# Self-attention scores of two heads in the upper and lower 64 rows of the TensorE array

## The chip, the cores and the metric

The kernel runs on one core of a Trainium2 chip. The metric is the device time of one execution in microseconds (us). The kernel before takes 815.65 us, the median of three runs (815.26 to 817.07).

## What is computed

One layer of an encoder for 512 tokens of width 1024: a token mixer, a cross-attention into 256 memory tokens and a gated MLP with a convolution, each between two RMS norms. The token mixer has two halves that run side by side: a recurrent group of four heads (HGRN2) and the self-attention group that this change touches. It has eight query heads of 64 elements that share two key and value heads, so heads 0 to 3 use the first key head and heads 4 to 7 the second:

```python
def axial_gqa_attention(q, k, v):
    ...
    scale = ATT_HEAD_DIM ** -0.5

    def one_block(qblk):
        s = jnp.einsum("bqhgd,bkhd->bhgqk", qblk, k).astype(jnp.float32) * scale
        p = jax.nn.softmax(s, axis=-1).astype(v.dtype)
        return jnp.einsum("bhgqk,bkhd->bqhd", p, v)
```

## The kernel before

**Splitting.** Matmul operands are kept as two fp32r tiles: `hi`, the value rounded by a cast on ScalarE (ACT), and `lo`, the rest, by a subtraction on VectorE (DVE) (`split`, L120 to L122). An ordinary product is then three matmuls, hi*hi, hi*lo and lo*hi (`mm3`, L277 to L280).

**Queries and keys.** `rope_q` (L770) writes for each block of 128 tokens and each head a row of 128 elements: 64 of `hi`, then 64 of `lo`. `turn_q` (L776) transposes them on TensorE (PE), so that `qT` holds one head in all 128 partitions, `hi` in the upper 64 and `lo` in the lower 64. The keys (`put_kv`, `turn_k`) are written twice, so that `kT` holds the same key `hi` (index c = 0) or the same key `lo` (c = 1) in both halves of the partitions.

**Attention** (L865 to L916) is a generator of 35 steps. Step i makes the scores of one head and one block of 128 queries: two matmuls with 128 rows and 512 columns into one PSUM bank `ps_s` (L872), which together give all four products of hi and lo. Then `softmax` (L847): the maximum of each row on DVE (L850), the exponential with its sum on ACT (L853), the reciprocal on DVE (L854), and the scaling, two times of three on ACT (L858), else on DVE (L860). Two steps later `turn(i - 2)` transposes the probabilities with four matmuls into a bank `ps_o` (L882), and `split` writes them as `hi` (ACT L121) and `lo` (DVE L122) to two `big` tiles of their head. When a head's four blocks are done, `weigh` (L885) multiplies them with the values, eight matmuls (L893), and ACT and DVE (L897, L898) write the result out.

**What sets the order.** `weave` (L73) interleaves three generators at L945 by the amounts that they yield: the last recurrent head (`hgrn_core(3)`), `attention`, and `attention_filler`. The filler is other PE work: the keys (`proj_fm`, 256 columns, banks `ps_b`, L278 to L280) and values of the cross-attention, and the first half of the output projection. From what is written in this order the framework's scheduler makes its own order for each engine, fixed when the kernel is built. Each engine works through its list in order, so a waiting instruction holds up all that stand behind it on that engine.

**Room.** There are two banks for each of the tags `s`, `o`, `b` and `c`, and 16 `big` buffers. A `big` tile is given room that an earlier tile has left; its first writer waits for the last reader of that tile. `hgrn_core(3)` has three such tiles: `qk` (queries and keys, multiplied in place, level by level), `tt` (the products of the gates) and `room`. For each of its levels it makes four matmuls into `ps_c` (L647; L654 at the level of 128), two multiplications on DVE (L673) and a masked copy (L679); then it transposes the keys (L659) and goes on with L664 and L685 to L687.

Of the kernel before, what the change touches and what calls it, by code (L numbers as in the profile page):

```python
# [10 lines left out]
F32R = mybir.dt.float32r  # L11
# [7 lines left out]
P = 128  # L19
D = 1024  # L20
T = 512
NB = T // P
# [67 lines left out]
def layer(tc, io, out):  # L90
    nc = tc.nc
# [13 lines left out]
    def small():  # L105
        return sm.tile([P, 16], F32, name="small", tag="small")

    def bank(tag):
        return ps.tile([P, 512], F32, name="ps_" + tag, tag=tag)

    def big(shape, dt=F32):
        return b8.tile(shape, dt, name="big", tag="big")

    def tmp2(shape=(P, 512), dt=F32, tag="ta"):
        return t2.tile(list(shape), dt, name="tmp2", tag=tag, bufs=TMP_BUFS[tag])

    def tmp4(shape, dt=F32):
        return t4.tile(shape, dt, name="tmp4", tag="tmp4")

    def split(hi, lo, src, eng=None):  # L120
        nc.scalar.copy(hi, src)  # L121
        (eng or nc.vector).tensor_sub(lo, src, hi.bitcast(F32))  # L122
# [159 lines left out]
    def blk(b):  # L282
        return slice(b * P, (b + 1) * P)
# [209 lines left out]
    for j in range(4):  # L493
# [8 lines left out]
        for k in range(2):  # L502
            kc = 2 * j + k
            for a, w in ((0, wh), (0, wl), (1, wh)):
                for b in range(NB):
                    nc.tensor.matmul(v_ps[b], hT.get(kc, blk(b))[a], w[:, half(k)],
                                     start=kc == 0 and a == 0 and w is wh, stop=kc == 7 and a == 1)
# [58 lines left out]
    def pair(act, i):  # L566
        t = big([P, 2, 2, T], F32R)
        act.hi[i], act.lo[i] = t[:, 0], t[:, 1]
# [200 lines left out]

    def rope_q(b, z):  # L770
        qr = norm_rope(z, 8, 0, b)
        qs = tmp4([P, 8, 2, 64], F32R)
        split(qs[:, :, 0, :], qs[:, :, 1, :], qr)
        return qs.rearrange("p h a d -> p h (a d)")

    def turn_q(b, q3):  # L776
        for g in range(2):
# [65 lines left out]
    kT, vv, qT = qkv["kT"], qkv["vv"], qkv["qT"]  # L843
# [3 lines left out]
    def softmax(s, n, width):  # L847
        s3 = s.rearrange("p (n k) -> p n k", n=n)
        mx = small()
        nc.vector.tensor_reduce(mx[:, :n], s3, axis=AX.X, op=ALU.max, negate=True)  # L850
        e = tmp2((P, n, width), tag="tq")
        for i in range(n):
            nc.scalar.activation(e[:, i, :], s3[:, i, :], ACT.Exp, bias=mx[:, i:i + 1], accum_out=mx[:, 2 + i:3 + i])  # L853
        nc.vector.reciprocal(mx[:, 4:4 + n], mx[:, 2:2 + n])  # L854
        for i in range(n):
            scaled[0] += 1
            if scaled[0] % 3:
                nc.scalar.mul(e[:, i, :], e[:, i, :], mx[:, 4 + i:5 + i])  # L858
            else:
                nc.vector.tensor_scalar(e[:, i, :], e[:, i, :], mx[:, 4 + i:5 + i], None, op0=ALU.mult)  # L860
        return e
# [3 lines left out]
    def attention():  # L865
        probs, pts, atts = {}, {}, {}

        def scores(i):
            h, qb = divmod(i, 4)
            s = bank("s")  # L870
            for c in range(2):
                nc.tensor.matmul(s, qT[h // 4][:, h % 4, blk(qb)], kT[:, 2 * (h // 4) + c, :],  # L872
                                 start=c == 0, stop=c == 1)
            probs[i] = softmax(s, 1, 512)

        def turn(i):
            if i % 4 == 0:
                pts[i // 4] = [big([P, 4, T], F32R) for _ in range(2)]
            (hi, lo), e = pts[i // 4], probs.pop(i)
            o = bank("o").rearrange("p (k n) -> p k n", k=4)  # L880
            for c in range(4):
                nc.tensor.transpose(o[:, c, :], e[:, 0, blk(c)], ident)  # L882
            split(hi[:, :, blk(i % 4)], lo[:, :, blk(i % 4)], o)

        def weigh(h):  # L885
            pt = pts.pop(h)
            if h % 2 == 0:
                atts[h // 2] = tmp2()
            att = atts[h // 2]
            o = bank("o")  # L890
            for c in range(4):
                for j in range(2):
                    nc.tensor.matmul(o, vv[:, c, h // 4].rearrange("p a d -> p (a d)"), pt[j][:, c, :],  # L893
                                     start=c + j == 0, stop=c == 3 and j == 1)
            low, high = slice(0, 64), slice(64, 128)
            dst, oth = (low, high) if h % 2 == 0 else (high, low)
            nc.scalar.copy(att[dst, :], o[oth, :])  # L897
            nc.vector.tensor_add(att[dst, :], o[dst, :], att[dst, :])  # L898
            if h % 2:
                if h % 4 == 1:  # L900
                    pair(mix, h // 4)
                split(*mix.get(h // 2, slice(0, T)), att)
                att_done[0] += 1

        n = 8 * NB
        yield ATT_LEAD
        while not turned[0]:
            yield None
        for i in range(n + 3):
            if i < n:  # L910
                scores(i)
            if 2 <= i <= n + 1:
                turn(i - 2)
            if i % 4 == 2 and i > 4:
                weigh(i // 4 - 1)
            yield 1.1  # L916

    def put_kx(c):
# [279 lines left out]
    rows = [small() for _ in range(NB)]  # L1198
# [148 lines left out]
```

## Time and profile before

| what | value |
|---|---|
| median of 3 runs | 815.65 us |
| profiled execution, first to last instruction (span) | 813.8 us |
| PE busy in the span | 803.3 us |
| DVE, ACT, POOL busy in the span | 574.7, 482.1, 136.9 us |
| first and last start of the score matmuls (L872) | 211.7 and 300.3 us |
| last start of the weighing matmuls (L893) | 308.9 us |

PE is a matmul, PEld a weight load beside it. A row of a timeline gives the start, the duration, the engine, the line, the operation, the tiles written and read, and the count. A row of a group gives the line, engine and operation, the tiles and shapes, the count, then the busy time in us with the mean of one in ns, then the idle time ahead of them with what ended it. The ends of matmuls are modelled and overlap the next start; what one costs PE is the distance from its start to the next one's. The profiled execution's own span is 1.85 us shorter than the median of the runs.

### The profile page before, as it was taken

What the parts mean: (1) busy time and instruction counts of PE and PEld (TensorE: products, weight loads), DVE (VectorE), ACT (ScalarE), POOL (GpSimd) and SP (SyncE); (2) the same over time, 40 slices, a digit from 0 to 9 for tenths busy, and PEclk for the clock granted to TensorE, in tenths of its full rate; (3) what the DMA queues carried; (4) which work ended last, traced back from release to release, by engine and by line L of the source; (5) the groups of instructions that cost most, each with busy time, mean ns of one, the idle gap of its engine ahead of it and who ended that gap; (6) DMA issues with size and microseconds to landing.
All of it is one profiled execution on the core that took longest, in us unless ns stands there. A gap on an engine that the chain in (4) does not pass through costs nothing.

```text
span 813.8 us, 11771 instructions
## 1 busy us (share of the span) xinstructions
PE 803.3 (99%) x4426; PEld 691.0 (85%) x4426; DVE 574.7 (71%) x868; ACT 482.1 (59%) x796; POOL 136.9 (17%) x213
## 2 busy tenths in 40 slices
PE   9999999999999999999999999999999999999996
PEld 7888888889998887888888898899999998888885
DVE  5456587469886865855453767987777788888765
ACT  5675757459988874644543553665555545566651
POOL 0111201053233102301010311211111111000301
PEclk9999999999999999999999999999999999999999
DMA  8685645569899753256634158776665677278852
GB/s 296 202 259 139 160 103 117 118 159 247 229 250 254 182 172 126 78 181 157 180 117 142 33 164 208 154 200 166 179 171 143 150 200 178 91 208 278 239 130 104
DMA packets 42457, 139.61 MB, mean 172 GB/s; under 512 B 5280, under 2 KB 6560, under 8 KB 42400
## 3 DMA queue, kind: packets, MB, share of 16 engines
q1 hardware_dynamic: 28944, 97.43, 35.5%
q0 software_dynamic: 12160, 38.54, 26.2%
q10 hardware_dynamic: 1296, 2.89, 1.0%
q8 instruction: 34, 0.56, 0.3%
q14 instruction: 23, 0.19, 0.1%
HBM read 135.17 MB, written 25.17 MB: 197 GB/s over the span
## 4 chain that ended last, share of the span: by engine, by line
PE 92%; DVE 3%; ACT 2%; issue 1%; POOL 1%; DMA 0%; DVEq 0%; POOLq 0%; SPq 0%; ACTq 0%
PE ps_b L279 10%; PE ps_b L280 10%; PE ps_b L278 10%; PE ps_s L278 6%; PE ps_s L280 6%; PE ps_s L279 6%; PE ps_o L278 5%; PE ps_o L279 5%; PE ps_o L280 5%; PE ps_c L278 5%; PE ps_c L280 5%; PE ps_c L279 5%; PE ps_c L647 3%; PE ps_o L893 2%; PE ps_s L872 2%; PE ps_o L882 2%
## 5 line engine op out<-in xcount | busy, mean ns | idle before, releaser
L222 ACT CAST wh<-raw 128x1024 fp32r<-128x1024 f32 x110 | 113.7, 1035 | 114.6 <-PE ps_b L279 35.3
L224 DVE TENSOR_TENSOR wl<-raw,wh 128x1024 fp32r<-128x1024 f32 (+1 forms) x77 | 92.3, 1201 | 72.2 <-ACT wh L222 72.0
L278 PE MATMUL ps_b<-big,wh 128*128 128x512 f32 (+1 forms) x344 | 122.3, 355 | 0.0
L280 PE MATMUL ps_b<-big,wl 128*128 128x512 f32 (+1 forms) x344 | 121.2, 352 | 0.0
L279 PE MATMUL ps_b<-big,wh 128*128 128x512 f32 (+1 forms) x344 | 121.2, 352 | 0.0
L280 PEld LDWEIGHTS ps_b<-big,wl 128*128 128x128 f32 x344 | 65.1, 189 | 8.5 <-DMA wl<-in_wu_dram 0.2
L278 PEld LDWEIGHTS ps_b<-big,wh 128*128 128x128 f32 x344 | 65.1, 189 | 8.3
L279 PEld LDWEIGHTS ps_b<-big,wh 128*128 128x128 f32 x344 | 65.1, 189 | 8.1
L673 DVE TENSOR_TENSOR big<-big 128x512 f32<-128x512 f32 x64 | 47.2, 755 | 9.6 <-PE ps_c L647 4.0
L278 PE MATMUL ps_s<-wh,big 128*128 128x512 f32 (+1 forms) x140 | 53.4, 383 | 0.0
L279 PE MATMUL ps_s<-wl,big 128*128 128x512 f32 (+1 forms) x140 | 53.3, 381 | 0.0
L280 PE MATMUL ps_s<-wh,big 128*128 128x512 f32 (+1 forms) x140 | 53.0, 379 | 0.0
L230 POOL DMA_DIRECT2D wl<-in_w_dram x33 | 29.3, 887 | 126.7 <-ACT wl L229 91.5
L122 DVE TENSOR_TENSOR big<-ps_o,big 128x512 fp32r<-128x512 f32 x54 | 36.9, 687 | 15.0 <-ACT big L121 13.4
L121 ACT CAST big<-ps_o 128x512 fp32r<-128x512 f32 x54 | 31.7, 588 | 18.5 <-PE ps_o L996 7.5
L278 PE MATMUL ps_s<-big,wh 128*128 128x256 f32 (+1 forms) x120 | 40.0, 334 | 0.0
L279 PE MATMUL ps_s<-big,wh 128*128 128x256 f32 (+1 forms) x120 | 40.0, 333 | 0.0
L280 PE MATMUL ps_s<-big,wl 128*128 128x256 f32 (+1 forms) x120 | 40.0, 333 | 0.0
L278 PE MATMUL ps_o<-wh,big 128*128 128x512 f32 (+1 forms) x102 | 39.2, 385 | 0.0
L279 PE MATMUL ps_c<-big,wh 128*128 128x256 f32 (+1 forms) x120 | 39.1, 326 | 0.0
L278 PE MATMUL ps_c<-big,wh 128*128 128x256 f32 (+1 forms) x120 | 39.1, 326 | 0.0
L280 PE MATMUL ps_c<-big,wl 128*128 128x256 f32 (+1 forms) x120 | 39.1, 326 | 0.0
(315 smaller groups left out, 2149.3 us busy)
## 6 DMA issues: line engine op xcount, KB each, us to landing
raw<-in_w_dram SPq DMA_DIRECT2D x91, 512.0 KB, 3.6
wl<-in_w_dram POOLq DMA_DIRECT2D x33, 512.0 KB, 7.3
sum_t<-in_wd_dram SPq DMA_DIRECT2D x20, 512.0 KB, 6.3
tmp<-in_wu_dram SPq DMA_DIRECT2D x14, 512.0 KB, 6.9
sum_t<-in_wd_dram POOLq DMA_DIRECT2D x10, 512.0 KB, 8.4
sum_t<-sum_t POOLq DMA_DIRECT2D x10, 512.0 KB, 7.5
big<-sum_t SPq DMA_DIRECT2D x10, 512.0 KB, 4.7
raw<-sum_t SPq DMA_DIRECT2D x10, 512.0 KB, 4.4
```

The lines of the kernel that those rows point to most:

```text
L121: nc.scalar.copy(hi, src)
L122: (eng or nc.vector).tensor_sub(lo, src, hi.bitcast(F32))
L222: nc.scalar.copy(wh, raw)
L224: last_low[0] = nc.vector.tensor_sub(wl[:, :by_dma], raw[:, :by_dma], wh[:, :by_dma].bitcast(F32)).ins
L230: nc.gpsimd.dma_start(wl[:, by_dma:], source(i)[:, by_dma:], accum_op=ALU.add)
L278: nc.tensor.matmul(o, a[0], b[0], start=start, stop=False, skip_group_check=again)
L279: nc.tensor.matmul(o, a[0], b[1], start=False, stop=False, skip_group_check=again)
L280: last_mm[0] = nc.tensor.matmul(o, a[1], b[0], start=False, stop=stop, skip_group_check=again).ins
L647: nc.tensor.matmul(o[:, b, :], kc[:, blk(b)], qc[:, blk(b)] if m == 1 else pat(qk, b * P, [[2 * m, P // (2 * m)], [T + m, 2], [1, m]]), st ...
L673: nc.vector.tensor_tensor(out=c, in0=c, in1=pat(tt, toff + off, [[2, npair], [gap, 2], [0, m]]), op=ALU.mult)
L872: nc.tensor.matmul(s, qT[h // 4][:, h % 4, blk(qb)], kT[:, 2 * (h // 4) + c, :], start=c == 0, stop=c == 1)
L882: nc.tensor.transpose(o[:, c, :], e[:, 0, blk(c)], ident)
```

## The change

- `rope_q` writes the rotated queries as all eight heads' `hi`, then all eight heads' `lo`, so that a row of 128 elements that `turn_q` transposes holds two heads. `qT[0]` then holds `hi` and `qT[1]` holds `lo`, each with head 2n in the upper 64 partitions and head 2n + 1 in the lower 64.
- `scores(i)` works on a pair of heads and one block of queries. It takes both `ps_s` banks, one for each head, and issues three products for each (hi*hi, hi*lo, lo*hi; lo*lo is left out), alternating between the heads. Each matmul has 64 rows and 512 columns; in the built program its array tile is 64x128, at row 0 for the first head and row 64 for the second. Every other matmul of the kernel keeps the 128x128 tile. There are 96 score matmuls where 64 were.
- `turn` and `weigh` work on the same amounts as before, but a pair of heads is in flight at once, so four `big` tiles of probabilities are made at the first block of a pair where two were made at the first block of a head. The turns come one step after the scores, one head ahead of the next scores and one behind them.
- The generator has 16 such steps and a last one, each yielding twice, and weighs the last two heads at its end.

```diff
--- before.py
+++ after.py
@@ -769,9 +769,9 @@
 
     def rope_q(b, z):
         qr = norm_rope(z, 8, 0, b)
-        qs = tmp4([P, 8, 2, 64], F32R)
-        split(qs[:, :, 0, :], qs[:, :, 1, :], qr)
-        return qs.rearrange("p h a d -> p h (a d)")
+        qs = tmp4([P, 2, 8, 64], F32R)
+        split(qs[:, 0], qs[:, 1], qr)
+        return qs.rearrange("p a (h two) d -> p (a h) (two d)", two=2)
 
     def turn_q(b, q3):
         for g in range(2):
@@ -866,17 +866,21 @@
         probs, pts, atts = {}, {}, {}
 
         def scores(i):
-            h, qb = divmod(i, 4)
-            s = bank("s")
-            for c in range(2):
-                nc.tensor.matmul(s, qT[h // 4][:, h % 4, blk(qb)], kT[:, 2 * (h // 4) + c, :],
-                                 start=c == 0, stop=c == 1)
-            probs[i] = softmax(s, 1, 512)
-
-        def turn(i):
+            n, qb = divmod(i, 4)
+            both = [bank("s") for _ in range(2)]
+            for a, c in ((0, 0), (0, 1), (1, 0)):
+                for k in range(2):
+                    rows = slice(64 * k, 64 * k + 64)
+                    nc.tensor.matmul(both[k], qT[a][rows, n, blk(qb)], kT[rows, 2 * (n // 2) + c, :],
+                                     start=a + c == 0, stop=a == 1)
+            for k in range(2):
+                probs[i, k] = softmax(both[k], 1, 512)
+
+        def turn(i, k):
+            h = 2 * (i // 4) + k
             if i % 4 == 0:
-                pts[i // 4] = [big([P, 4, T], F32R) for _ in range(2)]
-            (hi, lo), e = pts[i // 4], probs.pop(i)
+                pts[h] = [big([P, 4, T], F32R) for _ in range(2)]
+            (hi, lo), e = pts[h], probs.pop((i, k))
             o = bank("o").rearrange("p (k n) -> p k n", k=4)
             for c in range(4):
                 nc.tensor.transpose(o[:, c, :], e[:, 0, blk(c)], ident)
@@ -902,17 +906,25 @@
                 split(*mix.get(h // 2, slice(0, T)), att)
                 att_done[0] += 1
 
-        n = 8 * NB
+        n = 4 * NB
         yield ATT_LEAD
         while not turned[0]:
             yield None
-        for i in range(n + 3):
+        for i in range(n + 1):
+            if i % 4 == 1 and i > 4:
+                weigh(i // 2 - 2)
+            if i > 0:
+                turn(i - 1, 0)
             if i < n:
                 scores(i)
-            if 2 <= i <= n + 1:
-                turn(i - 2)
-            if i % 4 == 2 and i > 4:
-                weigh(i // 4 - 1)
+            yield 1.1
+            if i % 4 == 1 and i > 4:
+                weigh(i // 2 - 1)
+            if i > 0:
+                turn(i - 1, 1)
+            yield 1.1
+        for h in (6, 7):
+            weigh(h)
             yield 1.1
 
     def put_kx(c):
```

The order on three engines shows what the scheduler makes of this. In the names, `big_1159` holds the transposed keys, `big_1161` and `big_1162` the transposed queries, `big_1120` and `big_1121` the memory tokens, `ps_s` banks are told apart by number. First PE, a few us into the attention, with the score matmuls of the third block. Before, each bank has both its matmuls in one row:

```order
L872 MATMUL ps_s_2067<-big_1159,big_1161 128x512 x2
L279 MATMUL ps_b_2143<-big_1121,wh_1912 128x256
L872 MATMUL ps_s_2085<-big_1159,big_1161 128x512 x2
L280 MATMUL ps_b_2143<-big_1120,wl_1913 128x256
L278 MATMUL ps_b_2143<-big_1120,wh_1912 128x256
L882 MATMUL ps_o_2078<-ident_84,tmp2_2054 128x128 x4
```

Now, with the pair's two banks `ps_s_2131` and `ps_s_2132`:

```order
L874 MATMUL ps_s_2131<-big_1159,big_1161 128x512 x2
L874 MATMUL ps_s_2131<-big_1159,big_1162 128x512
L279 MATMUL ps_b_2160<-big_1121,wh_1912 128x256
L280 MATMUL ps_b_2160<-big_1120,wl_1913 128x256
L278 MATMUL ps_b_2160<-big_1120,wh_1912 128x256
L279 MATMUL ps_b_2160<-big_1121,wh_1912 128x256
L874 MATMUL ps_s_2132<-big_1159,big_1161 128x512
L886 MATMUL ps_o_2124<-ident_84,tmp2_2088 128x128 x4
L874 MATMUL ps_s_2132<-big_1159,big_1161 128x512
L874 MATMUL ps_s_2132<-big_1159,big_1162 128x512
```

The pair is not kept together here: the scheduler puts a matmul where its own bank comes free, so the first head's three stand ahead of the second head's three, with other work between. Of the 16 pairs, six alternate unbroken, two alternate with four transposes between them, four have three matmuls and then three (one of these with a weighing between and the order mixed at its end), and four are taken apart as here.

Second, PE where the last levels of `hgrn_core(3)` stand. Before, the level of 128 (L654) lies between the filler's matmuls:

```order
L279 MATMUL ps_b<-big,wh 128x256
L280 MATMUL ps_b<-big,wl 128x256
L654 MATMUL ps_c<-big 128x128 x4
L278 MATMUL ps_b<-big,wh 128x256
L279 MATMUL ps_b<-big,wh 128x256
L280 MATMUL ps_b<-big,wl 128x256
L278 MATMUL ps_b<-big,wh 128x256
L279 MATMUL ps_b<-big,wh 128x256
L280 MATMUL ps_b<-big,wl 128x256
L872 MATMUL ps_s<-big 128x512 x2
L882 MATMUL ps_o<-ident,tmp_2375 128x128 x4
```

Now the level of 64 (L647), the level of 128 and what follows stand one behind the other:

```order
L280 MATMUL ps_b<-big,wl 128x256
L647 MATMUL ps_c<-big,tmp_2351 128x128 x4
L654 MATMUL ps_c<-big 128x128 x4
L659 MATMUL ps_c<-ident,big 128x128 x4
L664 MATMUL ps_c<-big 128x128
L886 MATMUL ps_o<-ident,tmp_2141 128x128 x4
L664 MATMUL ps_c<-big 128x128
L886 MATMUL ps_o<-ident,tmp_2147 128x128 x4
L664 MATMUL ps_c<-big 128x128 x2
L685 MATMUL ps_c<-big 128x128
L874 MATMUL ps_s<-big 128x512
L886 MATMUL ps_o<-ident,tmp_2223 128x128 x4
```

The next filler matmul comes nine rows further down, behind the first weighing (L897). Moved here are the filler, which stood between these steps and is now used up ahead of them, and the turns of the third block (`tmp_2141`, `tmp_2147`), which now stand behind them.

Third, DVE at the same place. Before, the `lo` halves of the probabilities (`big_2380`, that head's) and the last level's multiplications (L673, in place on `qk`, which is `big_1411`, with the gates `tt`, which is `big_1412`) take turns:

```order
L673 TENSOR_TENSOR big_1411<-big_1411,big_1412 128x2x2x128
L854 RECIPROCAL small_2429<-small_2429 128x1
L122 TENSOR_TENSOR big_2380<-ps_o_2435,big_2379 128x4x128
L860 TENSOR_SCALAR tmp2_2431<-tmp2_2431,small_2429 128x512
L673 TENSOR_TENSOR big_1411<-big_1411,big_1412 128x2x2x128
L850 TENSOR_REDUCE small_2465<-ps_s_2462 128x1
L122 TENSOR_TENSOR big_2380<-ps_o_2471,big_2379 128x4x128
```

Now (`big_2099` is the `lo` tile of the second head, `big_2070` that of the first):

```order
L850 TENSOR_REDUCE small_2302<-ps_s_2294 128x1
L673 TENSOR_TENSOR big_1411<-big_1411,big_1412 128x4x2x64
L679 COPY_PREDICATED big_1849<-masks_299,ps_c_2353 128x4x128
L673 TENSOR_TENSOR big_1411<-big_1411,big_1412 128x2x2x128 x2
L122 TENSOR_TENSOR big_2099<-ps_o_2100,big_2098 128x4x128
L122 TENSOR_TENSOR big_2099<-ps_o_2176,big_2098 128x4x128
L122 TENSOR_TENSOR big_2070<-ps_o_2206,big_2069 128x4x128
```

The second head's `lo` halves have moved behind the last L673: in the built program `big_2099` lies at the address of `big_1412`, the gates, whose last reader is that L673. Until then the banks `ps_o_2100` and `ps_o_2176`, both that there are, stay taken. In the same way the second tile of cross-attention keys (`big_2159`) lies at the address of the first head's `hi` probabilities and waits for the first weighing, as it did before (there for the `lo` probabilities); that weighing stood behind the scores of 8 blocks of a head and now stands behind 11, and behind all these steps. Outside the stretch from the turning of the queries to the end of the attention, the lists of PE, DVE, ACT and POOL are the same as before; on SP one load of weights changes places with the loads of `x`.

## The prediction

> **What bounds the kernel now.** I read the page first, for the engine that has no room.
>
> ```profile
> span 813.8 us, 11771 instructions
> PE 803.3 (99%) x4426; PEld 691.0 (85%) x4426; DVE 574.7 (71%) x868; ACT 482.1 (59%) x796; POOL 136.9 (17%) x213
> PE 92%; DVE 3%; ACT 2%; issue 1%; POOL 1%; DMA 0%; DVEq 0%; POOLq 0%; SPq 0%; ACTq 0%
> ```
>
> PE is busy for 99% of the span, and 92% of the chain that ended last is PE. So an edit is worth what it takes from PE's list, or puts into it, waits included. Next the busy times of the attention's own stretch, from the first score matmul to the end of the last weighing, and the waits on PE from 211 to 311 us.
>
> ```profile
> 211.70:309.10 97.40, 97.04 (x574) 82.94 (x575) 72.85 (x144) 79.37 (x164) 20.54 (x23) 1.00 0.78 217
> PE ps_b L278 <- DVE big L122: 0.3, 1, 0.3
> ```
>
> After the stretch's length, the busy times are PE, PEld, DVE, ACT and POOL; then the clock, which is full. PE is idle for 97.40 - 97.04 = 0.36 us of 97, and one wait makes 0.3 of it. Nothing is to be won by better hiding. DVE and ACT, at 75% and 81%, have little slack: if their work bunches up, PE will wait.
>
> A busy PE is not yet a price, since matmuls overlap. The timeline gives prices, as distances between starts:
>
> ```profile
> 286.93 2.04 PE L893 MATMUL ps_o<-big,vv 128*128 128x512 f32 x8
> 288.81 0.39 PE L280 MATMUL ps_b<-wh,big 128*128 128x512 f32 x1
> 289.03 0.62 PE L872 MATMUL ps_s<-big 128*128 128x512 f32 x2
> 289.49 0.60 PE L882 MATMUL ps_o<-ident,tmp 128*128 128x128 f32 x4
> 289.85 0.48 PE L278 MATMUL ps_c<-wh,big 128*128 128x512 f32 x1
> 290.16 0.40 PE L279 MATMUL ps_c<-wl,big 128*128 128x512 f32 x1
> 290.40 0.39 PE L280 MATMUL ps_c<-wh,big 128*128 128x512 f32 x1
> ...
> 240.81 0.28 PE L279 MATMUL ps_b<-big,wh 128*128 128x256 f32 x1
> 240.93 0.28 PE L280 MATMUL ps_b<-big,wl 128*128 128x256 f32 x1
> 241.05 1.05 PE L654 MATMUL ps_c<-big 128*128 128x128 f32 x8
> 241.86 0.36 PE L278 MATMUL ps_b<-big,wh 128*128 128x256 f32 x1
> ```
>
> A score matmul costs (289.49 - 289.03) / 2 = 0.23 us, four transposes 0.36, a weighing 1.88, a filler matmul of 256 columns 0.12, four matmuls of the recurrence 0.81 (0.20 each; L647, L664, L685 and L686 are taken at this). The first matmul behind the transposes takes 0.31 to the next start where its kind takes 0.23 or 0.24: a change of kind costs some 0.08.
>
> **The slots of the score matmuls.** Before, 64 matmuls cost 64 x 0.23 = 14.7 us. After, there are 96 of half the rows. If a matmul in the upper rows and one in the lower run side by side, a pair of heads needs 3 slots in place of 4, 48 in all, and 3.7 us would be won. But by the order only neighbours can run side by side. A slot is counted where a score matmul follows one on the same rows, or follows other work. The six unbroken pairs need 3 slots each, 18. Those with three and then three share only the two in the middle: 5 each for four pairs, 20. The two with transposes between need 4 each, 8. The four that are taken apart need 6 each, 24. Sum 70, six more than before: 6 x 0.23 = +1.4 us. The edit's own arithmetic is gone before any wait is counted. No row of before has 64 rows or two matmuls side by side; from the nearest, L872, the other end is no overlap: 96 - 64 = 32 slots, +7.4 us. I take +1.4, since the two use different rows and banks.
>
> The Trainium skill ("TensorE: Matmul & The Clock Gate", "Part 3: Packing small matmuls — row/col tiling") has matmuls in distinct row groups start about 4 ns apart and run together, and starting in program order. By that the 70 stands; no row of before can show it.
>
> **Changes of tile.** The 96 stand in 26 groups, so PE goes from the 128x128 tile to the 64x128 one and back 52 times. Bounds from rows: nothing; or all that is in flight has to end first:
>
> ```profile
> L872 PE MATMUL ps_s<-big x64: 389/396/497, 211.7 to 300.3; 128*128 128x512 f32 x64
> ```
>
> The median of 396 ns less the 0.23 to the next start is 0.17. The nearest row is the change behind the transposes, 0.08, and I take that. Eleven groups stand ahead of where the filler resumes, in a stretch where PE will wait (below) and they hide; 15 groups are left: 30 x 0.08 = +2.4 us (0 to 30 x 0.17 = 5.1).
>
> The Trainium skill speaks against the change here ("TensorEngine Tiling (Array Packing)", "Tiling Modes"): changing the tiling mode, not merely the tile, drains the engine. It gives no figure; by that rule the term would stand at its upper end, 5.1, a rival below.
>
> **The waits where the recurrence ends.** The order shows that DVE writes the second head's `lo` only behind the last L673 of `hgrn_core(3)`, that both `ps_o` banks are held till then, and that the turns of the third block stand behind this on PE without filler between: two filler groups fill the `ps_b` banks, and the third waits for the weighing. When does DVE get there?
>
> ```profile
> L122 DVE TENSOR_TENSOR big<-ps_o,big 128x512 fp32r<-128x512 f32 x32 | 21.8, 685 | 7.3 <-ACT big L121 5.7 <-PE ps_o L893 1.4
> L850 DVE TENSOR_REDUCE small<-ps_s 128x1 f32<-128x512 f32 x32 | 21.7, 682 | 7.7 <-PE ps_s L872 7.4
> L673 DVE TENSOR_TENSOR big<-big 128x512 f32<-128x512 f32 x9 | 6.8, 755 | 1.2 <-PE ps_c L647 0.7 <-PE ps_c L654 0.4
> L854 DVE RECIPROCAL small<-small 128x1 f32<-128x1 f32 x32 | 5.0, 156 | 0.8 <-ACT tmp L853 0.6
> L860 DVE TENSOR_SCALAR tmp<-tmp,small 128x512 f32<-128x512 f32 x10 | 5.0, 499 | 0.2
> L679 DVE COPY_PREDICATED big<-masks,ps_c 128x512 f32<-128x512 uint8 x4 | 2.9, 734 | 0.0
> L122 DVE TENSOR_TENSOR big<-ps_b,big 128x256 fp32r<-128x256 f32 x5 | 2.1, 410 | 0.0
> ```
>
> From the first maximum to that first `lo`, DVE's new list has 9 L850 (6.14), 9 L673 (6.80), 4 L679 (2.94), 7 L854 (1.09), 2 L860 (1.00), 3 large L122 (2.06) and 1 of 256 columns (0.41): 20.4 us without a gap. It can start 0.9 us after the first score (three slots and 0.2 for the end of a matmul): 21.3. PE, up to the first turn behind L664, has 59 filler matmuls (7.1), 21 recurrence matmuls (4.2), the L659 transposes and 4 turns (1.8), and 20 score slots (4.6): 17.7 us. So PE waits 21.3 - 17.7 = 3.6 us, less what changes of kind take meanwhile. Before, the same level (L654) stood between filler at 241.05 us, 29 us after the first score, and nobody waited.
>
> Behind that, PE needs each turn's bank back through ACT and DVE, and the next scores' bank through the exponentials:
>
> ```profile
> L853 ACT ACTIVATE tmp<-ps_s,small 128x512 f32<-128x512 f32 x32 | 22.4, 699 | 1.8 <-DVE small L850 1.4 <-DVE small L854 0.2
> L121 ACT CAST big<-ps_o 128x512 fp32r<-128x512 f32 x32 | 18.8, 588 | 5.7 <-PE ps_o L882 4.7 <-PE ps_o L893 0.8
> L858 ACT ACTIVATE tmp<-tmp,small 128x512 f32<-128x512 f32 x22 | 16.0, 731 | 2.4 <-DVE small L854 2.3
> L853 ACT ACTIVATION_READ_ACCUMULATOR tmp<-ps_s,small 128x1 f32 x32 | 6.6, 208 | 0.0
> ```
>
> From the split of that first turn to the exponential whose bank the sixth pair's scores need, ACT's new list has three casts, two exponentials and one scaling: 3 x 0.588 + 2 x 0.907 + 0.731 = 4.3 us, behind a turn's 0.36 and 0.2 for its end: 4.9. PE's own work there is four turns, five recurrence matmuls and three score slots, 1.44 + 1.0 + 0.69 = 3.1 us. So 1.8 more. Together 5.4, and the changes of kind ahead take a little of it: I take +5.0 us. Bounds: 0 if the last levels are done early, 8 if the dependent steps L647, L673, L654, L673, L659 leave DVE gaps as well.
>
> A second place is where the rest of `hgrn_core(3)` (L687) frees `qk` for the second pair's `lo` tile of its second head: six turns, two weighings and most of two pairs of scores come within some 30 rows with 18 filler matmuls between. Behind a turn, ACT's cast and the exponential that frees the next scores' bank take 0.2 + 0.588 + 0.907 = 1.7 us, against a turn and four filler matmuls of 512 columns on PE, 0.36 + 4 x 0.23 = 1.3. Three such places make about +1.0 us (0 to 2).
>
> **What costs nothing.** The rotated queries' split writes another layout of the same size, four times on each engine:
>
> ```profile
> L122 DVE TENSOR_TENSOR tmp<-tmp,tmp 128x512 fp32r<-128x512 f32 x4 | 2.7, 687 | 0.0
> L121 ACT CAST tmp<-tmp 128x512 fp32r<-128x512 f32 x4 | 2.5, 618 | 0.5 <-DVE tmp L738 0.5
> ```
>
> The large L122 and L121 above, with plain layouts, take 685 and 588, so no more than four times 0.03 us could change, and filler covers it; without cover it is 0.1. Softmax, turns and weighings keep their number and size. POOL's list and SP's hardly move. At the end of the attention the last two weighings stand together, with the output projection's matmuls ahead and behind.
>
> **Sum.** +1.4 + 2.4 + 5.0 + 1.0 = +9.8 us. The profiled execution's span goes from 813.8 to 823.6. It lies 1.85 us under the median of the runs, and I keep that distance: 815.65 + 9.8 = 825.4.
>
> **Rivals.**
>
> *The halves do not run side by side.* Then 96 slots, 32 more instead of 6: 6.0 us more, 831.4. For it: no row shows two matmuls at once. Against it: separate rows and banks.
>
> *Every change of tile waits for the matmuls in flight.* 0.17 instead of 0.08 for 30 changes: 2.7 more, 828.1. For it: even a change of kind costs 0.08 here. Against it: nothing in the rows but that this 0.08 is half of it. (The rule on tiling modes in the Trainium skill, "TensorEngine Tiling (Array Packing)", names this case.)
>
> *The wait does not come, and the time is not slower.* Its place is the DVE list ahead of the first `lo` of the second head. If DVE reaches it within 17.7 us of the first score, PE finds the bank free, both waits fall away, and with free changes of tile only the slots are left, less the 0.36 idle now: 1.4 - 0.4 = +1.0, 816.7. For it: L850, L673 and L122 had idle time before them in the profile, so DVE was not full. Against it: the 20.4 us count no gap at all.
>
> That the pairing is not what the words of the change say is part of the forecast: the scheduler undoes it for ten of 16 pairs.
>
> **How the numbers follow.** The measurement can tell 0.2%, 1.6 us, from no change. The forecast has 0.50 (changes of tile from 0 to 0.08, waits from 4 to 8: 822 to 829). No overlap has 0.17, full draining 0.13, no wait 0.20. Around its 816.7 the last case spreads over 0.04 faster, 0.11 the same and 0.05 slower. So slower is 0.85, the same 0.11, faster 0.04. The range leaves out about half of the no-wait case below and half of the no-overlap case above: 816.5 to 832.
>
> **What would show it.** In the timeline, score matmuls of an unbroken pair should start in twos, with 0.23 us from one two to the next, and those of a pair taken apart 0.23 each. The distance at a change of tile should be 0.05 to 0.1 above its kind's. PE should have some 5 us of idle time between 15 and 30 us after the first score, ended by DVE L122 and ACT L853, and a little some 15 us later; the rest of its list should keep its prices. The forecast is wrong if PE's idle time in the attention stays below 1 us, if the pairs start 0.23 apart throughout, or if the time moves outside the attention.

## Result and the profile after

The kernel after takes 830.63 us, the median of four runs (829.83 to 832.24), beside 815.57 us for four runs of the kernel before (815.26 to 817.07). The ratio is 1.0179, with a 95% interval of 1.0167 to 1.0191: 15.06 us slower, where I forecast 9.8. The profiled execution's span grew from 813.8 to 828.0 us, by 14.2; it is the shortest of the four, and two of the others, of which no profile was kept, are 1.5 and 2.4 us longer. The top of its page and its chain first:

```profile
span 828.0 us, 11842 instructions
PE 815.5 (98%) x4458; PEld 690.5 (83%) x4458; DVE 574.4 (69%) x868; ACT 482.8 (58%) x796; POOL 137.2 (17%) x213
PE 92%; ACT 2%; DVE 2%; DMA 1%; issue 1%; POOL 0%; SPq 0%; DVEq 0%; POOLq 0%
```

PE still sets the time. Its busy time grew by 12.2 us (803.3 to 815.5); the other 2 us of the span are idle time of PE. DVE and ACT do what they did. Next the busy times by stretch, in the order PE, PEld, DVE, ACT, POOL, then the clock: the stretch shown of before, and 15 us around the place where I expected PE to wait.

```profile
211.70:309.10 97.40, 95.04 (x539) 71.83 (x539) 64.53 (x131) 71.75 (x149) 19.90 (x21) 1.00 0.69 183
225.00:240.00 15.00, 12.73 (x91) 10.36 (x87) 11.09 (x20) 9.40 (x18) 6.26 (x6) 1.00 0.92 242
```

PE is idle for 2.36 us of the first stretch (before: 0.36), and 2.27 of that lie in the second. The clock is full. The attention itself, by its score matmuls (L874) and its weighings (L897, before L893); the two times are the first and the last start:

```profile
L874 PE MATMUL ps_s<-big x96: 385/394/502, 212.1 to 311.4; 64*128 64x512 f32 x96
L897 PE MATMUL ps_o<-big,vv x64: 388/389/502, 241.7 to 323.4; 128*128 128x512 f32 x64
```

From the first score to the last weighing's start PE now needs 323.4 - 212.1 = 111.3 us, before 308.9 - 211.7 = 97.2. These 14.1 us are the loss of the profiled execution but for 0.1: the first score starts 0.3 us later than before, and what follows the last weighing's start is 0.3 us shorter. The timeline of PE shows both of its kinds:

```profile
211.75 0.28 PE L278 MATMUL ps_b<-big,wh 128*128 128x256 f32 x1
212.05 0.96 PE L874 MATMUL ps_s<-big 64*128 64x512 f32 x6
212.94 0.39 PE L279 MATMUL ps_b<-big,wh 128*128 128x256 f32 x1
213.17 0.28 PE L280 MATMUL ps_b<-big,wl 128*128 128x256 f32 x1
...
215.94 1.63 PE L874 MATMUL ps_s<-big 64*128 64x512 f32 x6
217.51 0.66 PE L886 MATMUL ps_o<-ident,tmp 128*128 128x128 f32 x4
...
230.91 1.06 PE L647 MATMUL ps_c<-big,tmp 128*128 128x128 f32 x8
232.75 1.16 PE L654 MATMUL ps_c<-big 128*128 128x128 f32 x8 [0.78 <-DVE big L673]
234.69 0.66 PE L659 MATMUL ps_c<-ident,big 128*128 128x128 f32 x4 [0.78 <-DVE big L673]
236.03 0.49 PE L664 MATMUL ps_c<-big 128*128 128x128 f32 x2 [0.68 <-ACT big L660]
236.35 0.60 PE L886 MATMUL ps_o<-ident,tmp 128*128 128x128 f32 x4
```

The first pair stands unbroken: its six matmuls take 0.89 us to the next start, three slots of 0.23 and 0.20 more. In the records the two of a slot mostly start 3 to 4 ns apart (2 to 17 ns over all 24 such pairs of matmuls). The Trainium skill says the same ("TensorE: Matmul & The Clock Gate", Part 3: about 4 ns between the starts of matmuls in different row groups). The group at 215.94 has three of one half and then three of the other, and takes 1.57: next to nothing is shared where the half changes only once. Two more such groups, at 256.74 and 286.31, take 1.52 and 1.44. The first filler matmul behind a group takes 0.23 to the next start where its kind takes 0.12. Then the recurrence: three waits of PE, ended by DVE (L673, twice) and ACT (L660). The turn (L886) behind them does not wait. DVE at the same time:

```profile
232.00 0.69 DVE L673 TENSOR_TENSOR big<-big 128x512 f32<-128x512 f32 x1 [0.72 <-PE ps_c L647]
...
233.95 1.29 DVE L673 TENSOR_TENSOR big<-big 128x512 f32<-128x512 f32 x2 [0.61 <-PE ps_c L654]
235.28 1.29 DVE L122 TENSOR_TENSOR big<-ps_o,big 128x512 fp32r<-128x512 f32 x2
```

DVE is not late. It waits for PE there (0.72 and 0.61 us), as PE waits for it: the steps hand over to each other, with no other work between. DVE begins the second head's first `lo` (L122) at 235.28, 23.2 us after the first score; the turn of PE that I had expected to wait for it starts at 236.35, 24.3 us after.

### The profile page after: what moved, and what is told of

It is laid out like the page before. It is cut to its first block, busy times and chain, and to the rows that moved or that the text cites. A ratio compares the mean times of both kernels' runs of the same rounds, so it can differ in the third digit from the quotient of the medians.

```text
span 828.0 us, 11842 instructions
## 1 busy us (share of the span) xinstructions
PE 815.5 (98%) x4458; PEld 690.5 (83%) x4458; DVE 574.4 (69%) x868; ACT 482.8 (58%) x796; POOL 137.2 (17%) x213
## 4 chain that ended last, share of the span: by engine, by line
PE 92%; ACT 2%; DVE 2%; DMA 1%; issue 1%; POOL 0%; SPq 0%; DVEq 0%; POOLq 0%
PE ps_b L278 10%; PE ps_b L279 10%; PE ps_b L280 9%; PE ps_s L278 7%; PE ps_s L280 7%; PE ps_s L279 7%; PE ps_o L278 5%; PE ps_o L280 5%; PE ps_o L279 5%; PE ps_c L278 4%; PE ps_c L280 4%; PE ps_c L279 4%; PE ps_c L647 3%; PE ps_s L874 2%; PE ps_o L886 2%; PE ps_o L897 2%
## 5 line engine op out<-in xcount | busy, mean ns | idle before, releaser
L673 DVE TENSOR_TENSOR big<-big 128x512 f32<-128x512 f32 x64 | 46.5, 746 | 10.9 <-PE ps_c L647 4.7
L122 DVE TENSOR_TENSOR big<-ps_o,big 128x512 fp32r<-128x512 f32 x54 | 36.7, 686 | 16.1 <-ACT big L121 15.3
```

The costliest lines, as they stand in the source:

```text
L673: nc.vector.tensor_tensor(out=c, in0=c, in1=pat(tt, toff + off, [[2, npair], [gap, 2], [0, m]]), op=ALU.mult)
```

## Experiments

**Theories.** A group is a run of score matmuls of 64 rows with nothing else between them on PE; after has 26. *Tile*: going to the 64-row tile and back is the main cost, about 0.2 us for each change and 0.41 for a group, as the distances in the trace suggest. *Order* (the rival): the new order of the steps, its waits and the room of its tiles are the main cost. Each time below is compared with runs of the kernel before on the same chip.

### One lone 64-row matmul in another stage

```diff
-  mm3(o, (w[0][:, kc, :], w[1][:, kc, :]), hT.get(kc, slice(0, T)), kc == 0, kc == 7)
+  a, b = (w[0][:, kc, :], w[1][:, kc, :]), hT.get(kc, slice(0, T))
+  if kc == 4:
+      nc.tensor.matmul(o, a[0], b[0], start=False, stop=False)
+      nc.tensor.matmul(o, a[0][:64], b[1][:64], start=False, stop=False)
+      nc.tensor.matmul(o, a[1], b[0], start=False, stop=False)
+  else:
+      mm3(o, a, b, kc == 0, kc == 7)
```

> The kernel before, in which one matmul of 512 columns in each of 26 units of the MLP's up projection uses 64 rows of the 128 (half of the rows' products of these 26 matmuls are left out); nothing else is changed, and the attention is that of before. It measures a group of one by itself, without the attention's order. Theory (0.41 us for a group, two changes of tile at 0.2): 26 x 0.41 = 10.7 above before, 826.3 (824 to 829). If a change costs 0.08, 4.2 above (819.8); if 0.17, 8.8 (824.4); if the cost in the attention came from waits and not from the tile, nothing (815.6).

Measured: 826.43 us (826.17 to 826.82), ratio 1.0130 (1.0115 to 1.0145), 10.7 us above before. That is 0.41 for each group, as *tile* has it. The timeline of PE at one of the 26 places:

```profile
492.43 0.39 PE L280 MATMUL ps_b<-big,wl 128*128 128x512 f32 x1
492.65 0.39 PE L1169 MATMUL ps_b<-big,wh 128*128 128x512 f32 x1
492.97 0.50 PE L1170 MATMUL ps_b<-big,wh 64*128 64x512 f32 x1
493.40 0.50 PE L1171 MATMUL ps_b<-big,wl 128*128 128x512 f32 x1
493.74 0.39 PE L278 MATMUL ps_b<-big,wh 128*128 128x512 f32 x1
```

The distances are 0.32, 0.43 and 0.34 where the kind takes 0.23. Each change lengthens two distances by about 0.1: that of the matmul ahead of it, and that of the first on the new tile. The Trainium skill ("TensorEngine Tiling (Array Packing)", "Tiling Modes") says that a change of mode drains the engine. The trace shows that a change costs something, 0.2 us here, and so agrees that far; it does not show a full drain, since the ends of matmuls are modelled and the first distance, 0.32, is shorter than the 0.39 that the matmul is given.

### Three 64-row matmuls in the same places

```diff
-  mm3(o, (w[0][:, kc, :], w[1][:, kc, :]), hT.get(kc, slice(0, T)), kc == 0, kc == 7)
+  rows = slice(0, 64) if kc == 4 else slice(0, 128)
+  hi, lo = hT.get(kc, slice(0, T))
+  mm3(o, (w[0][rows, kc, :], w[1][rows, kc, :]), (hi[rows], lo[rows]), kc == 0, kc == 7)
```

> The kernel before with the same 26 units of the up projection, but three matmuls of each in a row on 64 rows in place of one (half of their products are left out). Theory (the cost is that of going to the 64-row tile and back, whatever the number between): as with one matmul in each unit, 10.7 above before, 826.4. Rival (each 64-row matmul costs more by itself): three times that, 847.

Measured: 827.05 us (826.56 to 827.67), ratio 1.0135 (1.0120 to 1.0150): 11.1 above before, or 0.43 for a group of three. PE in one of them:

```profile
492.57 0.49 PE L278 MATMUL ps_b<-big,wh 64*128 64x512 f32 x1
492.90 0.39 PE L279 MATMUL ps_b<-big,wh 64*128 64x512 f32 x1
493.14 0.39 PE L280 MATMUL ps_b<-big,wl 64*128 64x512 f32 x1
493.46 0.50 PE L278 MATMUL ps_b<-big,wh 128*128 128x512 f32 x1
```

The matmul in the middle keeps 0.24. The cost belongs to the change, not to the matmul.

### The pairs' steps with scores of the whole array

The queries get their layout of before back (that part of the edit is left out here), and the loop of the scores becomes

```diff
   ...
+  for k in range(2):
+      h = 2 * n + k
+      for c in range(2):
+          nc.tensor.matmul(both[k], qT[h // 4][:, h % 4, blk(qb)], kT[:, 2 * (h // 4) + c, :],
+                           start=c == 0, stop=c == 1)
```

> The steps of the kernel after (pairs of heads, one turn ahead of the scores and one behind, four tiles of probabilities at a time), but each head's scores made as in the kernel before: two matmuls of 128 rows and 512 columns, lo*lo among them. So 64 score matmuls, no 64-row tile and no change of tile; the order of the steps and the room of the tiles are those of after. Theory (the change of tile is the main cost, about 0.2 us for each of 52 changes, and the order's waits cost about 3): 3 us above the kernel before, 818.6 (817.5 to 820). Rival (the order and its waits are the main cost): only the slots and some 0.08 for each change would go, so 10 us or more above before, 825 to 829.

Measured: 825.53 us (825.10 to 826.37), ratio 1.0120 (1.0105 to 1.0135), 9.8 above before. *Tile* expected 3; this looks like *order*. But the program is not after's without the tile: with fewer score matmuls the scheduler makes another list, 31 groups, with the filler used up earlier and two L647 side by side. PE in the cluster:

```profile
227.21 1.16 PE L647 MATMUL ps_c<-big,tmp 128*128 128x128 f32 x8 [0.25 <-ACT tmp L644]
230.18 1.88 PE L647 MATMUL ps_c<-big,tmp 128*128 128x128 f32 x8 [1.81 <-DVE big L673]
232.84 2.08 PE L654 MATMUL ps_c<-big 128*128 128x128 f32 x8 [0.78 <-DVE big L673]
```

and busy times by stretch, with the clock after POOL:

```profile
229.00:230.00 1.00, 0.00 (x0) 0.00 (x0) 1.00 (x2) 0.00 (x0) 0.70 (x2) 1.00 0.97 242
230.00:241.00 11.00, 8.57 (x39) 7.61 (x39) 6.00 (x11) 2.97 (x7) 0.65 (x1) 0.53 1.04 284
```

PE waits 1.81 us ahead of the second L647, and from then on the granted clock is half for some ten microseconds: the eight matmuls of L654 take 2.08 where 1.16 is usual. This run mixes three things and decides nothing. A test of the tile has to keep the order.

### Unbroken pairs, in halves and on the whole array

Edges between instructions hold each pair's matmuls together, so that PE has 16 groups. The edit for the scores, shortened; like edges hold the turns and the exponentials in their order:

```diff
+  with ExitStack() as stack:
+      if first or last_turn[0]:
+          stack.enter_context(tc.issue_after(first or last_turn[0]))
+      made = nc.tensor.matmul(...).ins
+      first = first or made
   ...
```

> The kernel after, with order edges that keep each of the 16 pairs together, six score matmuls alternating between the halves of the rows with nothing between: 48 slots, and 16 groups of 64-row matmuls in place of 26. Theory (0.41 us for a group, two changes of tile): 16 x 0.41 = 6.6, less 16 slots saved, 3.7, and waits of the order some 3: 5.9 above before, 821.5 (818 to 824), and 2.9 above the run with the same order and whole-array scores. Rival (changes cost nothing or 0.08 each): the 16 slots saved decide, and it is 1 to 3.7 us faster than that run.

> The order of the run with unbroken pairs, but with scores of the whole array as before: 16 groups of four matmuls of 128 rows, no change of tile. Theory: only the waits of this order are left, some 3 us: 818.6 (816.5 to 821), 2.9 below the unbroken pairs in halves. Rival (changes of tile are cheap): 1 to 3.7 us above the unbroken pairs in halves.

Measured: in halves 830.38 us (830.01 to 832.17), ratio 1.0185 (1.0168 to 1.0202); on the whole array 826.28 (825.63 to 826.32), ratio 1.0126 (1.0111 to 1.0141). Both missed their level, by 9 and 8 us. In part the edges make waits of their own (on PE: 1.5 us for ACT ahead of a turn in the first; three waits of together 1.4 us for DVE ahead of turns in the second): from 205 to 330 us PE is idle for 7.4 and 7.1 us, in before for 1.0. That is 6.4 and 6.1 where some 3 were expected, so about 5 us of each miss stay unexplained. The difference has the sign that *tile* gave, against the rival's: 4.1 us slower in halves, expected 2.9, although all 48 starts that can be shared are. The two lists are not the same, so I take no price from this.

### The same order, one tile or the other

These two keep every row of PE's, DVE's and ACT's order of after. The first has

```diff
-  rows = slice(64 * k, 64 * k + 64)
+  rows = slice(0, 128)
```

and, in the second, `rows = slice(0, 64)`.

> The kernel after with all 96 score matmuls over the 128 rows (each head's scores then contain the other head's products as well). The instructions of PE, DVE and ACT are those of after in the same order; only the tile of these matmuls differs, and so no two of them share a slot. Theory (0.41 us for a group of 64-row matmuls): 10.7 less for 26 groups, and 96 - 71 = 25 slots of 0.23 more, 5.7: 5 us below the kernel after, 825.6 (823.5 to 828, the upper part if PE's list, now shorter ahead of the recurrence's end, waits there longer). Rival (0.08 for a change of tile): 4.2 less and 5.7 more, 832.

> The kernel after with both heads' score matmuls in the upper 64 rows (the second head's scores are then made from the first head's rows). Order and changes of tile are those of after, but no two matmuls use different rows. Theory (matmuls of different rows share a slot where they stand next to each other, 25 times): 25 x 0.23 = 5.7 above the kernel after, 836.3 (834.5 to 838), and 10.7 above the run with the same order over 128 rows. Rival (the halves never ran side by side): as the kernel after, 830.6.

Measured: over 128 rows 827.43 us (827.25 to 828.46), ratio 1.0141 (1.0126 to 1.0156), 11.1 above before; both heads on the same 64 rows 834.38 (833.93 to 834.86), ratio 1.0222 (1.0205 to 1.0239), 18.0 above. Their first groups and their cluster on PE, and the starts of scores and weighings; first over 128 rows,

```profile
211.87 1.65 PE L874 MATMUL ps_s<-big 128*128 128x512 f32 x6
213.36 0.28 PE L279 MATMUL ps_b<-big,wh 128*128 128x256 f32 x1
...
231.75 1.16 PE L654 MATMUL ps_c<-big 128*128 128x128 f32 x8 [0.79 <-DVE big L673]
233.69 0.66 PE L659 MATMUL ps_c<-ident,big 128*128 128x128 f32 x4 [0.79 <-DVE big L673]
235.03 0.49 PE L664 MATMUL ps_c<-big 128*128 128x128 f32 x2 [0.68 <-ACT big L660]
```

```profile
L874 PE MATMUL ps_s<-big x96: 387/395/505, 211.9 to 308.8; 128*128 128x512 f32 x96
L897 PE MATMUL ps_o<-big,vv x64: 389/389/467, 240.4 to 320.6; 128*128 128x512 f32 x64
```

then on one half:

```profile
212.55 1.66 PE L874 MATMUL ps_s<-big 64*128 64x512 f32 x6
214.14 0.38 PE L279 MATMUL ps_b<-big,wh 128*128 128x256 f32 x1
```

```profile
L874 PE MATMUL ps_s<-big x96: 383/393/502, 212.6 to 316.4; 64*128 64x512 f32 x96
L897 PE MATMUL ps_o<-big,vv x64: 387/390/502, 243.6 to 328.4; 128*128 128x512 f32 x64
```

The six matmuls take 1.49 us over 128 rows and 1.59 on one half, 0.89 in after: the halves do run side by side, and a whole pair saves 0.70, three slots. From first score to last weighing's start the stretch takes 97.2 (before), 108.7 (after's order, 128 rows), 115.8 (one half), 111.3 us (after). So it can be laid out as steps:

| step | read from | us |
|---|---|---|
| slots of 32 more matmuls | 32 x 0.23 | +7.4 |
| the order | 108.7 - 97.2 - 7.4 | +4.1 |
| changes of tile | 115.8 - 108.7 | +7.1 |
| sharing | 111.3 - 115.8 | -4.5 |
| sum | 111.3 - 97.2 | +14.1 |

By the medians of the runs, each against its own before, the changes of tile cost 6.95 and sharing gives back 3.0 (18.0 - 15.1), since two of after's runs are longer than the profiled one. 24 starts are shared in after's records, worth 24 x 0.23 = 5.5, and the distances within the groups differ by just that; about 1 of it is lost again outside the groups, 0.3 of this as a wait of PE (L886 for ACT) that the one-half run, with its longer list, does not have. The first run lies in its range, the second just below it.

*Tile* had the signs right and the price of the changes too high here: 7.1, or 0.27 for a group, where 10.7 stood. Two things lower it. Over 128 rows these two waits of PE stand in the attention, and on one half they are gone:

```profile
PE ps_o L886 <- DVE big L122: 0.7, 1, 0.7
PE ps_s L874 <- ACT tmp L853: 0.2, 1, 0.2
```

The distances themselves grow by 8.1 us, 0.31 for a group: 2.4 ahead of the groups, 3.4 in them and 2.3 behind them. And the borders of a group partly coincide with a change of kind that costs PE something anyway: over 128 rows the first score of 17 of the 26 groups already takes 0.31 to 0.34 to the next start, where its kind takes 0.23.

### The change of tile in before's own attention

```diff
-  nc.tensor.matmul(s, qT[h // 4][:, h % 4, blk(qb)], kT[:, 2 * (h // 4) + c, :],
+  nc.tensor.matmul(s, qT[h // 4][0:64, h % 4, blk(qb)], kT[0:64, 2 * (h // 4) + c, :],
```

> The kernel before with its 64 score matmuls cut to the upper 64 rows (the other half of their products is left out: lo of the queries is not multiplied). The order of PE, DVE and ACT is that of before, and so are the tiles of probabilities; there are 32 groups of one to four 64-row matmuls. It measures the changes of tile at their place in the attention without the pairs. If a group costs what it cost in the up projection, 0.41: 32 x 0.41 = 13.1, 829 (827.5 to 830.5). If it costs what the same order showed between 64 and 128 rows, 6.95 / 26 = 0.27: 8.6, 824.6 (823.5 to 826). If 0.08 for a change: 5.1, 821.

Measured: 825.53 us (825.47 to 825.96), ratio 1.0117 (1.0102 to 1.0132): 9.6 above before, 0.30 for each of 32 groups, between the two expected prices and nearer to that of the attention. Its durations (least, median, most) and starts:

```profile
L872 PE MATMUL ps_s<-big x64: 386/443/501, 211.7 to 310.0; 64*128 64x512 f32 x64
L893 PE MATMUL ps_o<-big,vv x64: 387/392/497, 227.6 to 318.8; 128*128 128x512 f32 x64
```

The last weighing starts 318.8 - 308.9 = 9.9 us later. The median duration of a score matmul rose from 396 to 443 ns, and the list of waits has none on PE in the attention. Nothing but the tile differs from before, and it alone loses 1.2%.

### Later attention

```diff
-  CORE_SHARE, ATT_LEAD = 53.0, 4.0
+  CORE_SHARE, ATT_LEAD = 53.0, 9.0
```

> The kernel after with the attention's lead raised from 4 to 9 in the interleaving, so that it starts later beside the last recurrent head; the recurrence's last levels then stand between filler matmuls again, and the scores stand in 21 groups in place of 26. Theory: the waits at the recurrence's end go (2.8 us), five groups less are 2.0 us, and about as many slots: 4.8 below after, 825.8 (824 to 828). Rival (the waits only move to another place): 2.0 below after, 828.6.

> The pairs' steps with whole-array scores (64 matmuls of 128 rows, lo*lo included), with the attention's lead at 9 in place of 4. Without it, this program stood 9.8 above the kernel before, with 8 us of waits where the recurrence ends and ten microseconds of half the granted clock behind the longest of them. Theory (these waits come from the clustering alone, and the clock from the wait): both go, 816.5 (815.5 to 818.5). Rival (the pairs' room and turns cost by themselves, wherever they stand): 820 or more.

Measured: after with this edit 832.10 us (829.52 to 836.07), ratio 1.0200 (1.0164 to 1.0236), no better than after: the rival's side. Two of its four runs (829.52 and 830.21) had a granted clock of 0.998 and 0.999, the other two (833.99 and 836.07) 0.993, so the longer ones go with a lower clock; the two better ones, too, lie above the rival's 828.6. The pairs' steps on the whole array with it: 823.10 (822.00 to 823.95), ratio 1.0085 (1.0070 to 1.0100), 6.8 above before and 3.0 less above it than with the lead of 4; the clock stays full. Again the rival's side. In both the cluster is gone, and PE waits ahead of turns (L886) instead. The two longest waits of PE in the first:

```profile
PE ps_o L886 <- DVE big L122: 2.5, 2, 1.4
PE ps_o L886 <- DVE tmp L902: 1.7, 2, 1.5
```

Moving the whole attention trades the waits of one place for others. It does not tell whether the cluster causes those at its own.

### Three tiles of probabilities for a pair

```diff
-  pts[h] = [big([P, 4, T], F32R) for _ in range(2)]
+  pts[h] = [big([P, 4, T], F32R) for _ in range(2 - k)] + pts.get(h - k, [])[1:]
```

> The kernel after with three tiles of probabilities for a pair in place of four: both heads write their lo halves to the same tile (the first head's lo is overwritten by the second's). In this program no tile of probabilities lies in the room of the gates until the recurrence is done with them, and L647, L654, L659 and L664 stand apart again, with turns, weighings and scores between; the 26 groups and the products are those of after. Theory (the room of the fourth tile makes the cluster, and the cluster the waits of 2.8 us): 2.8 below the kernel after, 827.8 (826.5 to 829). Rival (the pairs' steps make the waits, wherever the recurrence stands): as the kernel after, 830.6.

> The run with three tiles for a pair, and all 96 score matmuls over the 128 rows: the same order of instructions, no change of tile, no shared slots. Theory: 32 more slots than in the kernel before, 7.4, and no wait: 823.1 (822 to 824.5), 2.8 to 4.3 below the run with after's order over 128 rows. Rival (the pairs' steps make the waits): 827, as that run.

Measured: 827.93 us (827.73 to 828.96), ratio 1.0148 (1.0133 to 1.0163), 12.0 above before where after is 15.1; over 128 rows 824.53 (824.27 to 825.64), ratio 1.0102 (1.0086 to 1.0119), 8.6 above where after's order over 128 rows is 11.1. The recurrence's steps on PE in the first run, apart again:

```profile
236.55 1.16 PE L654 MATMUL ps_c<-big 128*128 128x128 f32 x8
...
251.89 0.60 PE L659 MATMUL ps_c<-ident,big 128*128 128x128 f32 x4
...
254.60 0.71 PE L664 MATMUL ps_c<-big 128*128 128x128 f32 x4
```

None of them waits. The first run lies in the range of the theory, the second 0.03 us above its upper end. The starts of the two runs, halves and then 128 rows:

```profile
L874 PE MATMUL ps_s<-big x96: 385/394/502, 212.3 to 309.0; 64*128 64x512 f32 x96
L897 PE MATMUL ps_o<-big,vv x64: 387/391/502, 234.1 to 321.7; 128*128 128x512 f32 x64
```

```profile
L874 PE MATMUL ps_s<-big x96: 387/396/500, 213.2 to 306.9; 128*128 128x512 f32 x96
L897 PE MATMUL ps_o<-big,vv x64: 387/393/500, 234.5 to 319.3; 128*128 128x512 f32 x64
```

The stretch over 128 rows is 106.1 us, 97.2 + 7.4 + 1.5: the fourth tile makes the cluster and 2.5 (medians) to 2.6 (stretch) of the order's 4.1 us. In halves the same comparison gives 3.1 and 1.9. The other 1.5 us are not separated further. (The profiled execution over 128 rows, the longest of its four, also waits 0.8 us just ahead of its first score; the stretch does not contain this.)

## Why the prediction came out as it did

The forecast of slower, and the range, held; the middle was 5.2 us low. That the range held is partly luck. The forecast's own case was to give 822 to 829, and 830.6 lies above it, in the part that the range owed to the rival without overlap, which the runs refute. Three terms were off, in both directions: too little for the slots and the changes of tile, too much for the waits.

**Slots: right in mechanism, nearly in size.** I took +1.4 from 70 slots. The records share 24 starts, so 72 slots, nominally +1.8: of the four pairs with three matmuls and then three, I had let each share one start, and two share none. The steps above give 7.4 - 4.5 = +2.9, the rest being what is lost again outside the groups. That neighbours on different halves overlap is shown by the run on one half; that the order decides it, by the groups of six in after's records, 0.89 us where they alternate and 1.44 to 1.57 where they do not. The rival without overlap gave 831.4, the number nearest to the result, and is wrong all the same: without overlap the time is 834.4.

**Changes of tile: the step that failed.** "The nearest row is the change behind the transposes, 0.08, and I take that." In the up projection it measured 0.21 for each of two changes, above even my upper end of 0.17; in the attention 0.27 to 0.31 for a group, 0.14 to 0.16 for a change. A row of a change of kind on the same tile was no neighbour of a change of tile. The row that I kept for the bound, the 0.17 by which a matmul outlasts its start distance, was the better guide, and the rival that was priced by it had a chance of 0.13. My check, a distance 0.05 to 0.1 above its kind's, came out for each single distance (about 0.1 in the up projection), but I read one distance for a change; two are lengthened, ahead of it and behind it.

**"Eleven groups ... hide": wrong.** I left 22 of 52 changes out because PE would wait in that stretch. The runs show the waits of 0.78 (or 0.79), 0.78 and 0.68 us with the changes and without them, hardly a hundredth apart. In the orders with and without the cluster, halves cost 111.3 - 108.7 = 2.6 and 109.4 - 106.1 = 3.3 us more than 128 rows; by this the cluster's order covered some 0.7, and by the medians (4.0 and 3.4) nothing. With all 52 counted, my 0.08 would have given 4.2 of the 7.1; the price is the rest.

**Waits: the place right, the mechanism and the size not.** I forecast 5.0 where the recurrence ends and 1.0 near L687. The fourth tile costs about 2.5, and near L687 no wait shows. I had DVE reach the second head's `lo` late, after a backlog of 20.4 us that PE's 17.7 could not cover. In the trace DVE itself waits for PE, and the turn at 236.35 does not wait for a bank: my 17.7 us for PE up to there were 24.3, of which 2.2 are waits. The fourth tile acts earlier, when the order is made: with it the filler is used up and L647, L654, L659 and L664 stand one behind the other, with three tiles they do not. (That the scheduler does so because it finds no room is my reading; no run shows its choices.) Each of the last three then waits for the step between (L673, L673, L660). Such a wait is a latency: the work ahead of it, the changes of tile included, did not hide it in any of the three runs. I had named that chain only in the bound. The check that the idle time be "ended by DVE L122 and ACT L853" fails with it; PE's idle time in the 15 us was 2.3 us, not some 5.

**What cost nothing** cost nothing: the split with the new layout has means of 679 and 614 ns (before 687 and 618), and the time outside the attention is the same within 0.3 us on either side.

So 2.9 + 7.1 + 4.1 = 14.1 us in the attention, where 1.4 + 2.4 + 6.0 = 9.8 stood. No kernel tried here beats the one before.

## What to carry to other kernels

Count the groups of row-tiled matmuls in the built order before counting the slots that they save. Here a pair on two halves saves one slot against two whole-array matmuls for each head, 0.23 us, and going to the 64-row tile and back costs 0.27 to 0.43. By these numbers each trip must hold at least two pairs to gain anything, which this kernel's two banks for scores do not allow. When two versions are compared to price one cause, hold the order of every engine the same; a version with less work gets another schedule, and its waits can exceed what it saves.

## What was not expected of the hardware

- A change between the 128-row and the 64-row tile costs about 0.2 us in a stream of 512-column matmuls (0.41 to 0.43 for there and back, with one or with three matmuls between), and 0.14 to 0.16 beside transposes and other changes of kind.
- Three matmuls on one half and then three on the other take 1.44 to 1.57 us, little less than six on the same half (1.59); alternating, the six take 0.89.
- The granted clock fell to half for some ten microseconds behind a wait of 1.81 us. Waits of 1.5 and 0.8 us in the other runs left it full. The Trainium skill ("TensorE: Matmul & The Clock Gate", Part 1) names an idle window of about 3.4 us for this. PE did not pause that long here; whether the sparse matmuls ahead of the wait counted as idle was not tried.
